# Thirteen units per MLP in place of twelve, with the residual normed and added to in place

## The chip, the core and the metric

The kernel runs on one core of a Trainium2 chip. Its engines are TensorE (PE in the profile, with its weight loads as PEld), VectorE (DVE), ScalarE (ACT), GpSimd (POOL) and SyncE (SP), which issues the loads. The metric is the device time of one execution in microseconds. Each run reports the median of several executions.

## The reference

Sixteen meta tokens and 512 input tokens (528 rows of 1024) go through two layers. Each layer has a mixer and an MLP, and each of these ends in a residual and a LayerNorm:

```python
def sq_relu_mlp(h, w1, w2):
    return jnp.square(jax.nn.relu(h @ w1)) @ w2

    h = layer_norm(DN_ALPHA * h + mix, ln1_w[i], ln1_b[i])
    h = layer_norm(DN_ALPHA * h + sq_relu_mlp(h, mlp_w1[i], mlp_w2[i]), ln2_w[i], ln2_b[i])
```

`w1` is 1024 x 4096 and `w2` 4096 x 1024. The mixer of the first layer is retention and gated DeltaNet heads with one output projection, that of the second is Mamba-2. All is float32. The output drops the meta tokens.

## The kernel before

Activations lie transposed, features on the 128 partitions and tokens along the row. `h` is eight tiles of 528 tokens. In the first layer the tokens are cut in halves of 272 and 256, in the second (the meta tokens are no longer needed) in 256 and 256. Each matrix operand is split in a high part (a rounded copy, by ScalarE, L152) and a low part (the rest, by VectorE, L153), and a product is three matmuls: high by high, high by low, low by high (`mm3`, L172 to L174). In the second layer these run over all 512 tokens at once, and over 256 only where the halves are kept apart (`head` and `tail` of `phase`).

An output projection adds its product to `alpha * h` in a tile of its own (`residual`, L362 to L367). Here `h` is there as a high and a low part, so a first addition is two instructions on VectorE. `norm_after` transposes these sums, norms them by rows, transposes them back, and writes the new `h` as high part (ScalarE, L337), a float32 tile (VectorE, L339) and the low part from both (GpSimd or VectorE, L340).

The MLP's 4096 hidden features are eight groups of four tiles of 128. Per group: `h @ w1`, relu and square (L433 to L442), then the product with the group's rows of `w2`, added to the residual (L362). Groups 2 to 7 do the first product in `Unit`s. A unit takes two tiles of `w1` and both halves of the tokens and both halves of the 1024 inputs, as a product of 2 x 2 blocks, and does it with seven block products in place of eight, at the price of sums and differences of the blocks. One unit is 84 matmuls of half the tokens (L500), against 96. The sums of weight blocks are made in the unit (s1 to s4, L473 to L477), those of `h` once per MLP (`combos`, L385 to L401, split at L152 and L153), in 16 tiles. In the profile's names `m` are tiles of 272 columns (24 buffers), `s` tiles of 528 (40), `w` weight tiles (12), `pmm` and `pmx` PSUM tiles (3 and 5 banks).

The order of the work is that of the program: functions written as generators (`combos`, a unit's preparation, the norm) are advanced a step at each `tick` between products, and a scheduler then sets each engine's queue, in which instructions run in order. Groups 0 and 1 are done tile by tile: four tiles of group 0, then each tile of group 1 followed by two tiles of group 0's second product, whose weights are loaded as they are needed. During these the sums over `h` are made. Then units of two tiles and `Four`s (four tiles of a second product, their weights loaded and split one stage ahead) take turns, and group 7's second product ends the MLP tile by tile, the last three tiles with their halves apart (`tail=3`), so that the first half's norm can start. In the last norm (`finish`) the rows go out to memory.

Of the kernel before, what the change touches and what calls it, by code (L numbers as in the profile page):

```python
# [57 lines left out]
def trunk(ctx: ExitStack, tc: tile.TileContext, a, out):  # L58
# [250 lines left out]
    def norm_after(r, ns, wcol, bcol):  # L309
# [5 lines left out]
        def task(hf):  # L315
# [11 lines left out]
            for m in range(KT):  # L327
# [10 lines left out]
                t = tl("m", n)  # L338
# [33 lines left out]
    def combos(pairs, nh, get):  # L372


        q = slice(0, nh), slice(nh, 2 * nh)

        def part(k, c, lo):
            return pairs[k][lo][:, q[c]].bitcast(F32)

        def diff(out, a, b, engine):  # L380
            engine.tensor_tensor(out, a, b, op=SUB)

        for k in range(4):
            d1, d3, e = tl("m", nh), tl("m", nh), tl("m", nh)
            G.tensor_tensor(d1, part(k, 1, 0), part(k, 0, 0), op=SUB)  # L385
            V.tensor_tensor(e, part(k, 1, 1), part(k, 0, 1), op=SUB)
            V.tensor_tensor(d1, d1, e, op=ADD)
            get(0, k, d1)
            yield
            G.tensor_tensor(d3, part(k + 4, 1, 0), part(k, 1, 0), op=SUB)  # L390
            V.tensor_tensor(e, part(k + 4, 1, 1), part(k, 1, 1), op=SUB)
            V.tensor_tensor(d3, d3, e, op=ADD)
            get(2, k, d3)
            yield
            d2, d4 = tl("m", nh), tl("m", nh)
            G.tensor_tensor(d2, part(k + 4, 1, 0), d1, op=SUB)
            V.tensor_tensor(d2, d2, part(k + 4, 1, 1), op=ADD)
            get(1, k, d2)
            yield
            G.tensor_tensor(d4, part(k + 4, 0, 0), d2, op=SUB)  # L400
            V.tensor_tensor(d4, d4, part(k + 4, 0, 1), op=ADD)  # L401
            get(3, k, d4)
            yield

    def mlp(l, hx, ns, ready, r, evac0, pairs):
# [41 lines left out]

        def second(c, u, m0, m1, tail=0):
            phase([([lambda m=m: wload(second_src(c, m), 512)], m) for m in range(m0, m1)], u,
                  lambda m, hf, o: evac0(m, hf, o, last=c == NG - 1), ns, tail=tail)  # L450
# [110 lines left out]
        u, ev = group()  # L561
        phase([([w1[l, f]], f) for f in range(GF)], hx, ev, ns, head=3, ready=ready)
        spawn(combos(pairs, nh, get))
        stages = []
        un, evn = group()
        groups = [(u, ev), (un, evn)] + [group() for _ in range(2, NG)]
        for c in range(2, NG):
# [947 lines left out]
```

## Time and profile before

| | us |
|---|---|
| median of three runs (1734.0 to 1739.5) | 1738.64 |
| the profiled execution | 1738.46 |
| its span, first to last instruction | 1736.7 |
| TensorE busy | 1674.2 (96%) |
| VectorE busy | 1199.8 (69%) |
| ScalarE busy | 700.9 (40%) |
| GpSimd busy | 351.1 (20%) |
| mean granted clock of TensorE | 0.982 |

The first MLP is from about 535 to 918 us of the span, the second from about 1365 to the end, with the last norm behind it. Busy time on TensorE is pipelined: matmuls overlap, and what counts is how often one starts. "PEclk" is the granted clock as a share of full speed. A wait "X <- Y" is idle time of X before an instruction that Y released. In the tables by stretch each engine has its busy time in us and in brackets the number of instructions that ended or ran in it.

### The profile page before, as it was taken

The numbers are of one execution on the slowest core, as the hardware profiler recorded it, in microseconds if no ns is written. First come the engines' busy times: TensorE is split into PE (matmuls) and PEld (weight loads), VectorE is DVE, ScalarE is ACT, GpSimd is POOL, SyncE is SP. The second block draws the span as 40 slices with busy tenths as digits, with TensorE's granted clock in tenths as the row PEclk, the third lists the DMA queues.
The fourth block names the chain that finished last, engine by engine and source line by source line (L and its number), as shares of the span: only waits on it lengthen the run. The fifth ranks groups of instructions, "written<-read, shape, count | busy, mean of one in ns | idle before, by whom it ended". The sixth has DMA issues, their size and how long they took to land.

```text
span 1736.7 us, 30064 instructions
## 1 busy us (share of the span) xinstructions
PE 1674.2 (96%) x11896; PEld 1542.2 (89%) x11896; DVE 1199.8 (69%) x2383; ACT 700.9 (40%) x1354; POOL 351.1 (20%) x412
## 2 busy tenths in 40 slices
PE   9998999999999899999999998999999998999997
PEld 7897998899999889999998987888778987888886
DVE  5896666766437877767747876767564688777765
ACT  4432235554214344444424643545432434444431
POOL 1211210010003411111102145344410342111112
PEclk9998999999999999999999999999999999999999
DMA  7223212112222232222221443333223123222321
GB/s 243 82 91 86 88 47 84 46 54 84 87 74 68 73 104 98 98 98 98 79 71 62 137 121 92 102 112 98 91 67 110 55 91 110 98 98 98 101 73 69
DMA packets 93002, 158.05 MB, mean 91 GB/s; under 512 B 14077, under 2 KB 47229, under 8 KB 92605
## 3 DMA queue, kind: packets, MB, share of 16 engines
q1 hardware_dynamic: 92716, 155.87, 27.9%
q8 instruction: 93, 1.52, 0.4%
q14 instruction: 49, 0.39, 0.1%
q10 hardware_dynamic: 144, 0.26, 0.0%
HBM read 149.95 MB, written 6.15 MB: 90 GB/s over the span
## 4 chain that ended last, share of the span: by engine, by line
PE 79%; DVE 10%; DMA 4%; POOL 3%; ACT 2%; issue 2%; SPq 0%; POOLq 0%; DVEq 0%; ACTq 0%
PE pmm L172 18%; PE pmm L174 18%; PE pmm L173 18%; PE pmx L500 10%; PE pmm L500 4%; DVE w L153 2%; DVE s L603 2%; DMA row<-rd 1%; DMA w<-in_w 1%; PE pmx L1241 1%; PE pmx L270 1%; DMA du<-row 1%; POOL n L147 1%; PE pmx L1245 1%; ACT w L152 1%
## 5 line engine op out<-in xcount | busy, mean ns | idle before, releaser
L172 PE MATMUL pmm<-hh,w 128*128 128x256 f32 (+5 forms) x1528 | 472.9, 310 | 5.6 <-DVE m L366 2.8
L174 PE MATMUL pmm<-hh,w 128*128 128x256 f32 (+5 forms) x1528 | 459.4, 301 | 2.1 <-DVE w L153 2.1
L173 PE MATMUL pmm<-hl,w 128*128 128x256 f32 (+5 forms) x1528 | 458.4, 300 | 0.7 <-POOL hl L340 0.3
L153 DVE TENSOR_TENSOR w<-w,w 128x1024 fp32r<-128x1024 f32 (+2 forms) x269 | 323.7, 1205 | 142.0 <-PE pmm L173 67.6
L152 ACT CAST w<-w 128x1024 fp32r<-128x1024 f32 (+2 forms) x269 | 263.7, 981 | 373.7 <-PE pmm L174 137.1
L172 PE MATMUL pmm<-s,w 128*128 128x256 f32 (+2 forms) x1180 | 376.8, 319 | 4.3 <-DVE m L366 2.7
L174 PE MATMUL pmm<-s,w 128*128 128x256 f32 (+2 forms) x1180 | 375.5, 318 | 0.2 <-DVE w L153 0.2
L173 PE MATMUL pmm<-s,w 128*128 128x256 f32 (+2 forms) x1180 | 375.5, 318 | 0.0
L172 PEld LDWEIGHTS pmm<-hh,w 128*128 128x128 f32 (+2 forms) x1528 | 289.1, 189 | 20.9 <-issue 4.0
L173 PEld LDWEIGHTS pmm<-hl,w 128*128 128x128 f32 (+2 forms) x1528 | 289.0, 189 | 13.5 <-issue 2.4
L174 PEld LDWEIGHTS pmm<-hh,w 128*128 128x128 f32 (+2 forms) x1528 | 289.0, 189 | 11.4 <-DVE w L153 2.9
L172 PEld LDWEIGHTS pmm<-s,w 128*128 128x128 f32 x1180 | 222.3, 188 | 20.1 <-DVE m L366 3.2
L174 PEld LDWEIGHTS pmm<-s,w 128*128 128x128 f32 x1180 | 222.2, 188 | 15.8 <-DVE w L153 0.6
L173 PEld LDWEIGHTS pmm<-s,w 128*128 128x128 f32 x1180 | 222.2, 188 | 15.2 <-DVE s L1320 0.3
L435 POOL TENSOR_TENSOR m<-m 128x256 f32<-128x256 f32 (+2 forms) x128 | 89.0, 697 | 511.7 <-ACT m L433 499.4
L362 DVE TENSOR_TENSOR m<-m,pmm 128x256 f32<-128x256 f32 (+1 forms) x236 | 93.6, 416 | 71.7 <-PE pmm L174 71.5
L147 POOL TENSOR_TENSOR n<-n,neg 128x1 f32<-128x1 f32 (+2 forms) x58 | 39.8, 690 | 450.4 <-DVE n L146 426.4
L603 DVE SCALAR_TENSOR_TENSOR s<-s,pp,s 128x528 f32<-128x528 f32 x120 | 101.3, 844 | 33.4 <-ACT s L601 31.1
L442 DVE TENSOR_TENSOR s<-m,s 128x256 fp32r<-128x256 f32 (+2 forms) x128 | 69.5, 546 | 51.1 <-POOL m L435 49.9
L500 PE MATMUL pmx<-s,s 128*128 128x264 f32 (+1 forms) x576 | 75.4, 287 | 5.6 <-ACT s L152 5.3
L500 PEld LDWEIGHTS pmx<-s,s 128*128 128x128 f32 x576 | 72.5, 192 | 6.1 <-ACT s L152 5.5
L500 PE MATMUL pmx<-s,w 128*128 128x264 f32 (+1 forms) x576 | 77.6, 284 | 0.0
(312 smaller groups left out, 2368.1 us busy)
## 6 DMA issues: line engine op xcount, KB each, us to landing
w<-in_w SPq DMA_DIRECT2D x88, 512.0 KB, 3.3
w<-in_mw SPq DMA_DIRECT2D x176, 256.0 KB, 3.0
w<-in_mw SPq DMA_DIRECT2D x40, 512.0 KB, 3.2
w<-in_wo SPq DMA_DIRECT2D x29, 512.0 KB, 3.4
row<-rd SPq DMA_DIRECT2D x16, 512.0 KB, 5.7
s<-rd SPq DMA_DIRECT2D x32, 128.0 KB, 5.5
out<-row SPq DMA_DIRECT2D x7, 256.0 KB, 2.0
w<-in_wo SPq DMA_DIRECT2D x6, 256.0 KB, 2.5
```

The source lines that it names most:

```text
L147: G.tensor_tensor(dst, t, neg5[0:part, 0:n], op=POW)
L152: S.copy(dst_hi, src)
L153: V.tensor_tensor(dst_lo, src, dst_hi.bitcast(F32), op=SUB)
L172: T.matmul(o, w[0], x[0], start=first, stop=False)
L173: T.matmul(o, w[0], x[1], start=False, stop=False)
L174: T.matmul(o, w[1], x[0], start=False, stop=last)
L270: T.transpose(pt[m // 4][:bn, (m % 4) * P:(m % 4 + 1) * P], r[m][:, off:off + bn], ident)
L362: V.tensor_tensor(t, t, o, op=ADD)
L435: G.tensor_tensor(q, t, t, op=MUL)
L442: V.tensor_tensor(lo, q, hi.bitcast(F32), op=SUB)
L500: T.matmul(o, w[x][:, c], B[b][k][y], start=first and k == i == 0, stop=last and k == 3 and i == 2, skip_group_check=True)
L603: V.scalar_tensor_tensor(acc, cin[:, k:k + L], w[k], acc, op0=MUL, op1=ADD)
```

## The change

- `norm_after` writes the normed float32 tile over the residual sum that it normed, so that from an output projection to the end of its MLP `h` stays in the same 16 `m` tiles in float32.
- The MLP's residual (`accumulate`) adds to these tiles in place: a first addition is one instruction (`alpha * h + o`), later ones are an addition as before.
- `combos` takes its differences from the float32 tiles, all on VectorE. With halves of 272 and 256 the four token blocks are cut at 264, so a block can lie in two tiles and a difference can be two instructions, one of them 8 columns wide. GpSimd has no part in it.
- In group 1 only tiles 0 and 2 are done directly, one after the other; tiles 1 and 3 are a thirteenth unit. Group 0's second product becomes two `Four`s behind that unit. The later stages follow as before.
- Group 7's second product takes the weights of two `Four`s that are prepared ahead, and keeps the halves of the last four tiles apart (`tail=4`).

```diff
@@ norm_after
-                t = tl("m", n)
+                t = r[hf][m]
                 V.tensor_scalar(t, pf, w, b, op0=MUL, op1=ADD)
@@
+    def accumulate(h):
+        r, seen = [{}, {}], set()
+
+        def evac(m, hf, o, last=True):
+            t = h[hf][m]
+            if (m, hf) in seen:
+                V.tensor_tensor(t, t, o, op=ADD)
+            else:
+                V.scalar_tensor_tensor(t, t, DN_ALPHA, o, op0=MUL, op1=ADD)
+                seen.add((m, hf))
+            if last:
+                r[hf][m] = t
+        return r, evac
+
+    def combos(h, ns, nh, get):
+        def quarter(k, c):
+            a, b = h[0][k], h[1][k]
+            if c == 0:
+                return [(0, nh, a[:, 0:nh])]
+            cut = ns[0] - nh
+            return ([(0, cut, a[:, nh:ns[0]])] if cut else []) + [(cut, nh, b)]
+
+        def diff(out, x, y):
+            if not isinstance(y, list):
+                y = [(0, nh, y)]
+            for o, e, ap in x:
+                for o2, e2, ap2 in y:
+                    lo, hi = max(o, o2), min(e, e2)
+                    if lo < hi:
+                        V.tensor_tensor(out[:, lo:hi], ap[:, lo - o:hi - o], ap2[:, lo - o2:hi - o2], op=SUB)
         for k in range(4):
...
+            q0, q1 = [[quarter(i, c) for c in range(2)] for i in (k, k + 4)]
+            d = [tl("m", nh) for _ in range(4)]
+            diff(d[0], q0[1], q0[0])
+            diff(d[2], q1[1], q0[1])
+            diff(d[1], q1[1], d[0])
+            diff(d[3], q1[0], d[1])
+            for j in range(4):
+                get(j, k, d[j])
+                if j % 2:
+                    yield
@@ mlp
-        for c in range(2, NG):
-            for i in range(2):
-                stages.append(Unit(c, i, lambda f, hf, o, e=groups[c][1]: e(f, hf, o, nh)))
-                stages.append(Four(c - 1, groups[c - 1][0], 4 * i))
-        for f in range(GF):
-            phase([([w1[l, GF + f]], f)], hx, evn, ns)
-            if f == 2:
-                spawn(stages[0].gen)
-            second(0, u, 2 * f, 2 * f + 2)
+        stages = [unit(1, 1), four(0, 0), four(0, 1)]
         for c in range(2, NG):
+            stages += [unit(c, 0), four(c - 1, 0), unit(c, 1), four(c - 1, 1)]
+        last = [four(NG - 1, 0), four(NG - 1, 1)]
...
+        phase([([w1[l, f]], f) for f in range(GF)], hx, groups[0][1], ns, head=3, ready=ready)
+        spawn(combos(h, ns, nh, get))
+        phase([([w1[l, GF]], 0)], hx, groups[1][1], ns)
+        spawn(gens[0])
+        phase([([w1[l, GF + 2]], 2)], hx, groups[1][1], ns)
...
-        second(NG - 1, groups[-1][0], 0, KT, tail=3)
+        blks = last[0].blks + last[1].blks
+        phase([([[blks[m]]], m) for m in range(KT)], groups[-1][0], evac0, ns, tail=4)
@@ both layers
-    h = hn
-    r, ev = residual(h, (0, 0), ns0)
+    h, r0 = hn, r
+    r, ev = accumulate(r0)
```

Behind `combos` the lines of the changed kernel have higher numbers: L442 is L455 there, L473 to L477 are L482 to L486, L500 is L509; the sums' differences are L404, the first residual addition L381.

More of the change, by code (lines that the diff above doesn't have):

```diff
@@ L370, in residual @@
         return r, evac
[L372 to L381, printed above, removed]
-        for k in range(4):
[L384 to L403, printed above, removed]
@@ L409, in mlp @@
+    def mlp(l, hx, h, ns, ready, evac0, pairs):
         w1, w2 = a["mw1"], a["mw2"]
@@ L446, in second_src @@
             return w2[l, c // 2, m][:, c % 2 * 512:c % 2 * 512 + 512]
-        def second(c, u, m0, m1, tail=0):
-            phase([([lambda m=m: wload(second_src(c, m), 512)], m) for m in range(m0, m1)], u,
-                  lambda m, hf, o: evac0(m, hf, o, last=c == NG - 1), ns, tail=tail)
         class Unit:
@@ L559, in run, with unit, four @@
                             adv()
[L561 to L566, printed above, removed]
-        for c in range(2, NG):
-            for i in range(2):
-                stages.append(Unit(c, i, lambda f, hf, o, e=groups[c][1]: e(f, hf, o, nh)))
-                stages.append(Four(c - 1, groups[c - 1][0], 4 * i))
-        for f in range(GF):
-            phase([([w1[l, GF + f]], f)], hx, evn, ns)
-            if f == 2:
-                spawn(stages[0].gen)
-            second(0, u, 2 * f, 2 * f + 2)
+        groups = [group() for _ in range(NG)]
+        def unit(c, i):
+            return Unit(c, i, lambda f, hf, o: groups[c][1](f, hf, o, nh))
+        def four(c, i):
+            return Four(c, groups[c][0], 4 * i)
+        stages = [unit(1, 1), four(0, 0), four(0, 1)]
+        for c in range(2, NG):
+            stages += [unit(c, 0), four(c - 1, 0), unit(c, 1), four(c - 1, 1)]
+        last = [four(NG - 1, 0), four(NG - 1, 1)]
+        gens = [st.gen for st in stages + last]
+        phase([([w1[l, f]], f) for f in range(GF)], hx, groups[0][1], ns, head=3, ready=ready)
[3 more added lines that the diff above has]
+        phase([([w1[l, GF + 2]], 2)], hx, groups[1][1], ns)
         until(lambda: "s4" in stages[0].ops and all(x is not None for y in tt for x in y))
@@ L578, in mlp @@
               [half(k, 1) for k in range(4, 8)], tt[3], tt[0], tt[1], tt[2]]
-        next(stages[1].gen)
+        next(gens[1])
         for i, st in enumerate(stages):
-            nxt = stages[i + 1].gen if i + 1 < len(stages) else iter(())
-            if i + 2 < len(stages):
-                next(stages[i + 2].gen)
+            if i + 2 < len(gens):
+                next(gens[i + 2])
             def adv():
-                next(nxt, None)
+                next(gens[i + 1], None)
                 tick()
             st.run(adv)
-            for _ in nxt:
+            for _ in gens[i + 1]:
                 pass
-        second(NG - 1, groups[-1][0], 0, KT, tail=3)
+        for _ in gens[-1]:
+            pass
+        blks = last[0].blks + last[1].blks
+        phase([([[blks[m]]], m) for m in range(KT)], groups[-1][0], evac0, ns, tail=4)
     def conv_evac(cin, hf, o):
@@ L1365, in trunk @@
     phase([(srcs[m], m) for m in range(3, KT)], yw, ev, ns1, tail=1)
-    h = hn
-    r, ev = residual(h, (0, 0), ns1)
+    h, r0 = hn, r
+    r, ev = accumulate(r0)
     normed = [False, False]
```

5 lines of the change are left out of this document (2 added, 3 removed).

## The prediction

> **What bounds the kernel now.** I read the page first, then busy time by stretch at the head of each MLP, then what TensorE waited for there, then the rows of those stretches in order of time.
>
> ```profile
> PE 1674.2 (96%) x11896; PEld 1542.2 (89%) x11896; DVE 1199.8 (69%) x2383; ACT 700.9 (40%) x1354; POOL 351.1 (20%) x412
> PE 79%; DVE 10%; DMA 4%; POOL 3%; ACT 2%; issue 2%; SPq 0%; POOLq 0%; DVEq 0%; ACTq 0%
> ```
>
> TensorE is the bound nearly everywhere. A change pays by taking matmuls away or by closing the few places where TensorE stands still.
>
> ```profile
> core 0: us, PE busy (x) PEld busy (x) DVE busy (x) ACT busy (x) POOL busy (x), PEclk, DMA share, GB/s
> 640.00:680.00 40.00, 40.00 (x330) 40.00 (x329) 28.77 (x51) 15.05 (x27) 4.46 (x7) 1.00 0.27 93
> 566.87:627.57 60.70, 51.35 (x387) 49.70 (x385) 49.94 (x96) 22.21 (x47) 22.01 (x25) 0.94 0.24 77
> 590.00:600.00 10.00, 8.55 (x68) 8.13 (x67) 10.00 (x23) 3.84 (x9) 4.36 (x6) 1.00 0.01 2
> 614.32:619.21 4.89, 4.89 (x23) 4.89 (x23) 1.62 (x2) 0.00 (x0) 0.00 (x0) 0.51 0.16 54
> 1391.05:1436.06 45.01, 44.81 (x194) 35.97 (x193) 39.90 (x80) 18.92 (x42) 20.51 (x22) 1.00 0.30 100
> ```
>
> The first row is the steady middle of the first MLP: 330 matmuls in 40 us, 0.121 us each, no gap. The second is its head, from the first tile of group 1 to the first of the twelve units: 384 matmuls by the code, which at 0.121 us are 46.5 us, took 60.7. So 14.2 us were lost. Where they were lost VectorE was full (10.00 of 10 us), and then the clock stood at 0.51 for 4.9 us.
>
> ```profile
> PE pmm L172 <- DVE m L366: 5.6, 5, 1.5
> PE pmm L174 <- DVE w L153: 1.9, 1, 1.9
> PE pmm L172 <- ACT m L433: 1.6, 1, 1.6
> PE pmx L330 <- DVE row L322: 0.9, 1, 0.9
> PE pmx L330 <- ACT row L321: 0.7, 1, 0.7
> PE pmx L500 <- ACT s L152: 5.3, 1, 5.3
> PE pmx L270 <- DVE m L362: 1.8, 1, 1.8
> ```
>
> These are TensorE's waits: the first five in 560 to 930 us (first MLP and the norm behind it), the last two from 1350 us on. L366 is the first residual addition of a tile: VectorE is too late to free a PSUM bank. The 5.3 us is the second MLP's first unit, waiting for the last of the h sums. The 1.8 us lies at the very end.
>
> **The change, part by part.** *Matmuls.* A unit does two tiles of w1 in 84 matmuls of half width instead of 96. One more unit per MLP takes 12 away. Rows that give the pitch in the second MLP and mark the stretches:
>
> ```profile
> 566.87 0.29 PE L172 MATMUL pmm<-hh,w 128*128 128x272 f32 x1
> 572.74 0.29 PE L172 MATMUL pmm<-s,w 128*128 128x272 f32 x1
> 614.32 0.43 PE L172 MATMUL pmm<-hh,w 128*128 128x272 f32 x1
> 614.54 0.43 PE L173 MATMUL pmm<-hl,w 128*128 128x272 f32 x1
> 1391.05 0.39 PE L172 MATMUL pmm<-hh,w 128*128 128x512 f32 x1
> 1396.60 0.39 PE L172 MATMUL pmm<-s,w 128*128 128x512 f32 x1
> 1436.06 0.28 PE L500 MATMUL pmm<-hh,w 128*128 128x256 f32 x1
> 1437.36 0.28 PE L500 MATMUL pmm<-hh,w 128*128 128x256 f32 x1
> 1442.93 0.79 PE L500 MATMUL pmx<-s,s 128*128 128x256 f32 x2 [5.30 <-ACT s L152]
> 1444.00 2.50 PE L500 MATMUL pmx<-s,s 128*128 128x256 f32 x10 [0.27 <-DVE s L153]
> 1442.93:1447.15 4.22, 3.95 (x16) 3.65 (x17) 4.22 (x10) 2.79 (x5) 0.00 (x0) 0.50 0.00 0
> ```
>
> A direct tile of the first MLP takes 572.74 - 566.87 = 5.87 us. In the second MLP 24 matmuls of 512 take 5.55 us (0.231 each) and 12 of 256 start 11 pitches in 1.30 us (0.118). At the low clock the pitch is 0.22 in place of 0.12.
>
> The new head of the first MLP has two direct tiles, one unit and all of group 0's second products: 96 + 84 + 192 = 372 matmuls, 45.1 us. In the second it is 48 + 96 = 144 wide ones (33.3 us) and 84 of 256 (9.9 us), 43.2 us.
>
> *VectorE's chain in front of the unit.* Before, the sums over h had the whole head as cover, mixed with 32 residual instructions (L366 and L367) per MLP and 16 subtractions on GpSimd. Now one instruction per tile half does the residual, it stands behind the unit, and the sums are VectorE's alone. But the unit comes after only two direct tiles. Its product s2 needs the second sum of all four k, and the low part of s2. On VectorE, the end of that run in the first MLP (`s_7095` is the last sum it needs, `s_7099` the low part of s2):
>
> ```order
> L153 TENSOR_TENSOR s_7095<-m_7082,s_7095 128x264
> L153 TENSOR_TENSOR w_7164<-w_7120,w_7163 128x1024
> L153 TENSOR_TENSOR s_7099<-w_7009,s_7098 128x512
> L153 TENSOR_TENSOR s_7102<-m_7083,s_7102 128x264
> L153 TENSOR_TENSOR s_7105<-m_7084,s_7105 128x264
> ```
>
> In the kernel before, residual additions and just-in-time weight splits stood between the unit's own preparations at this place:
>
> ```order
> L477 TENSOR_TENSOR s_7387<-w_7360,w_7363 128x512
> L367 SCALAR_TENSOR_TENSOR m_7409<-hl_6432,m_7409 128x272
> L366 SCALAR_TENSOR_TENSOR m_7427<-hh_6431,pmm_7414 128x256
> L153 TENSOR_TENSOR w_7437<-w_7434,w_7436 128x1024
> L367 SCALAR_TENSOR_TENSOR m_7427<-hl_6432,m_7427 128x256
> ```
>
> These rows have moved behind the unit or are gone. On TensorE, the changed kernel does a11, four matmuls of group 0, a12, and then stands at s2 (`pmx_7133`):
>
> ```order
> L509 MATMUL pmm_7132<-hh_6444,w_7078 128x264
> L509 MATMUL pmx_7133<-s_6910,s_7098 128x264 x2
> L174 MATMUL pmm_7269<-s_6559,w_7164 128x272
> L172 MATMUL pmm_7269<-s_6651,w_7163 128x272
> ```
>
> The third matmul of s2 needs `s_7099`. What VectorE's instructions cost (two of POOL beside them):
>
> ```profile
> 546.72 0.14 DVE L146 TENSOR_SCALAR n<-n 128x1 f32<-128x1 f32 x1
> 546.78 0.15 DVE L306 SCALAR_TENSOR_TENSOR n<-n,n 128x1 f32<-128x1 f32 x1
> 571.35 0.98 DVE L442 TENSOR_TENSOR s<-m,s 128x272 fp32r<-128x272 f32 x1 [2.38 <-POOL m L435]
> 575.58 0.98 DVE L392 TENSOR_TENSOR m<-m,m 128x264 f32<-128x264 f32 x1
> 582.39 0.42 DVE L386 TENSOR_TENSOR m<-hl 128x264 f32<-128x264 f32 x1
> 582.73 0.43 DVE L367 SCALAR_TENSOR_TENSOR m<-hl,m 128x272 f32<-128x272 f32 x1
> 603.33 1.21 DVE L153 TENSOR_TENSOR w<-w,w 128x1024 fp32r<-128x1024 f32 x1
> 611.37 0.68 DVE L477 TENSOR_TENSOR s<-w,w 128x512 f32<-128x512 f32 x1
> 1398.96 0.95 DVE L442 TENSOR_TENSOR s<-m,s 128x256 fp32r<-128x256 f32 x1 [0.51 <-POOL m L435]
> 575.34 0.94 POOL L396 TENSOR_TENSOR m<-hh,m 128x264 f32<-128x264 f32 x1
> ```
>
> A half-width instruction starts every 0.35 us (0.42 long), but takes 0.98 beside a GpSimd one. 512 columns cost about 0.6, 1024 about 1.14. For the eight-column slivers, which the trace lacks, the nearest row is the 128x1 with a pitch of 0.06; with a wait for the row before it perhaps 0.16; I take 0.1.
>
> First MLP: group 1's first tile starts at 566.87 and its first low part at 571.35, 4.48 later. The second tile starts at 572.74, so its own is at 577.2 and done at 577.6. Behind it up to `s_7099` stand 22 half-width rows (11 sums, 10 splits, 1 evacuation), 7 slivers, two of 512 and one of 1024: 7.7 + 0.7 + 1.2 + 1.1 = 10.7, so 588.3. TensorE ends the tile at 578.6; a11, a12 and the four matmuls are 3.4 us, some 0.3 goes on a weight cast queued behind an activation: 582.3. Two matmuls of s2 and five others hide 0.85. The wait is 5.2 us. With four GpSimd squarings each stretching a row by 0.55 it is 7.4; I take 6.4. The clock then falls as after 614, 23 matmuls at 0.1 us too much, 2.4. So 45.1 + 0.3 + 6.4 + 2.4 = 54.2 against 60.7: **6.5 us won**.
>
> Second MLP: no slivers. The second low part of the first tile is at 1398.96 to 1399.9, 8.85 after the tile's start; for the next tile that is 1405.45. Then 15 half-width rows, two of 512 and one of 1024, 7.4: 1412.9. TensorE, from 1402.15, has a11, a12, four wide and here twenty more wide matmuls, 8.4 us, and two of s2: 1410.8. The wait is 2.1, with slow rows 3.5; I take 2.75, and half a clock drop, 1.0. Before: 45.0, then 5.57 of waits and over 4 us at a clock of 0.50, some 20 matmuls at 0.1 too much, 2.0: 52.6. After: 43.2 + 3.75 = 46.95. **5.6 us won**.
>
> The Trainium skill ("TensorE: Matmul & The Clock Gate", Part 1) says that the clock halves after an idle window of about 3.4 us, and that the window is free-running. By it alone the second MLP's gap would cost no clock, and the sum would be 1.0 better. The trace is harsher: before the low clock at 614 the longest single wait was 1.9 us, and several of them did it.
>
> *The last group.* Its weights are loaded and split as pairs ahead, and four tiles instead of three do their second halves last. So 12 matmuls of 256 (1.4 us) move behind the first half's norm. At the first MLP's end the waits on L322 and L321 were 0.9 + 0.7; the 1.4 us stand ahead of them now and leave about 0.25: **1.35 won**. At the program's end VectorE gets to the last two additions 1.4 us earlier, with one addition more in front (0.35): **1.1 won**, less 0.05 for the twice 256 columns.
>
> *At nothing:* the norm's writing into the sums' own tiles (their transposes are done); 16 `m` buffers held longer, since the other 8 served the same traffic before, from the residuals' start (if activations had to wait for GpSimd's 0.65 to 0.95, three free PSUM banks cover it); the same bytes of weights in fewer splits.
>
> Sum: 6.5 + 5.6 + 1.35 + 1.05 = 14.5. The profiled execution is 1738.46 (span 1736.7), the median 1738.64. **Forecast 1724 us.**
>
> **The rivals.** (a) *The clock holds* in both heads, and the low clock after the first MLP disappears. Against it are the gap of over 5 us and the low clock from 1442.93 behind one of 5.3. The gain is 2.4 + 1.0 and some 3 more: 1718.
> (b) *The slow form rules*: waits at 7.4 and 3.5, plus 2 us each for ScalarE's casts, which alternate with VectorE's splits, and a full clock drop in both. That takes 1.0 + 0.75 + 4 + 1.0: 1731.
> (c) *The wait only moves*: 6.5 and 5.6 us more of it than I count eat both heads' gain and leave 2.4: 1736, no change. For it speaks that VectorE was the late engine there before, too; against it that it loses 32 rows and GpSimd's company.
> (d) *Slower, by the weights.* On VectorE the unit's first differences of weights now stand in the same queue ahead of the sums, and wait for two loads whose buffers come free only as TensorE finishes the tiles of group 0. In this stretch the weights came none too early:
>
> ```profile
> 558.35 0.62 ACT L152 CAST w<-w 128x512 fp32r<-128x512 f32 x1 [2.03 <-DMA w<-in_mw]
> 569.62 0.62 ACT L152 CAST w<-w 128x512 fp32r<-128x512 f32 x1 [1.72 <-DMA w<-in_mw]
> ```
>
> If the two land 10 us behind the last evacuation of group 0 in both MLPs, every sum moves by that much or a little more: with 24 us in all, 24 - 14.5 makes it 1748. It decides from about 7 us per MLP. Against it: each of these casts had stood idle for 2 us only.
>
> **How the numbers follow.** Forecast 48%, (a) 20%, (b) 20%, (c) 7%, (d) 5%. What a measurement can tell from no change is 0.3%, 5.2 us: below 1733.4 is faster. Forecast and (a) are, and nearly all of (b): 0.87; same 0.08; slower 0.05. The range leaves out half of (a)'s better end, (c) and (d): 1715 to 1733.
>
> **What would show it.** Right: no wait on the residual additions in the heads, one wait of 5 to 7 us at the first unit's s2 in the first MLP and one of 2 to 3.5 in the second, waits at L330 behind the first MLP nearly gone, 12 matmuls fewer per MLP. Wrong: a wait at s2 over 10 us, VectorE idle at the first weight difference, or a new gap in the second products, where the residual additions and the next unit's preparation now meet.

## The result, and the profile after

The changed kernel took 1722.36 us, the median of four runs (1720.05 to 1724.06), against 1736.56 (1734.0 to 1739.5) before: ratio 0.9917, 95% interval 0.9894 to 0.994. A second set of four runs, beside other kernels, gave 1724.21 and 0.9926 (0.9901 to 0.9951). The forecast was 1724, range 1715 to 1733. The profiled execution was the fastest of its four, 1720.05 us with a span of 1718.3, so its 18.4 us against the profile of before are more than the 14.2 between the medians. The profile of the second set is its fastest run too (1719.78, in a set that reaches to 1727.63), so what follows from these two profiles shows the change at its best.

Busy time and the chain by engine, from the page of the changed kernel:

```profile
PE 1663.8 (97%) x11932; PEld 1535.2 (89%) x11932; DVE 1177.9 (69%) x2355; ACT 702.2 (41%) x1346; POOL 325.2 (19%) x380
PE 82%; DVE 7%; DMA 3%; POOL 3%; ACT 2%; issue 2%; SPq 0%; POOLq 0%; DVEq 0%; ACTq 0%
```

VectorE has 28 rows and 21.9 us of work less, GpSimd 32 rows and 25.9 us. VectorE's share of the chain of waits fell from 10 to 7%. TensorE's rows are 36 more: a unit in the second MLP puts 84 matmuls of 256 columns in the place of 48 of 512 (9.9 us in place of 11.1), one in the first 84 in the place of 96, and 12 wide ones of the last group are now 24.

TensorE's waits, first from 535 to 935 us (first MLP and the norm behind it), then from 1350 us on; columns are total, times, longest, in us:

```profile
PE pmx L509 <- ACT s L152: 3.2, 1, 3.2
PE pmx L330 <- ACT row L321: 0.9, 1, 0.9
PE pmx L330 <- DVE n L306: 0.9, 2, 0.5
PE pmm L173 <- POOL hl L340: 0.8, 2, 0.6
PE pmm L174 <- DVE w L153: 0.7, 1, 0.7
...
PE pmx L509 <- DVE s L153: 1.3, 1, 1.3
PE pmx L509 <- ACT s L152: 1.1, 1, 1.1
PE pmm L173 <- POOL hl L340: 1.0, 1, 1.0
PE pmx L270 <- DVE m L379: 0.9, 2, 0.6
```

In the heads no wait stands on the first residual addition any more. A wait at the first unit's s2 (L509) has come, 3.2 us in the first MLP and 2.4 in the second. Two rows are new that the prediction does not have: matmuls of group 0 that wait for a low part of the norm (`hl`, L340) from GpSimd, 0.8 and 1.0 us.

The first MLP's head by stretch: all of it, as in the row of before that starts at 566.87 (its columns are named there), and four microseconds behind the wait:

```profile
565.39:617.91 52.52, 47.88 (x374) 46.95 (x373) 40.03 (x94) 23.15 (x48) 7.53 (x9) 0.97 0.31 101
586.00:590.00 4.00, 3.61 (x19) 3.62 (x20) 4.00 (x8) 2.31 (x6) 0.00 (x0) 0.59 0.35 108
```

The head is 52.5 us long in place of 60.7, VectorE busy for 40 us in place of 50, and the clock falls behind the wait, but only for about 3 us.

The rows of TensorE, ScalarE and VectorE at s2, each in order of time:

```profile
579.29 0.39 PE L172 MATMUL pmm<-s,w 128*128 128x272 f32 x1 [0.53 <-ACT w L152]
580.23 0.39 PE L509 MATMUL pmm<-hh,w 128*128 128x264 f32 x1 [0.19 <-ACT row L513]
585.18 0.51 PE L509 MATMUL pmx<-s,s 128*128 128x264 f32 x2 [3.23 <-ACT s L152]
586.39 0.59 PE L174 MATMUL pmm<-s,w 128*128 128x272 f32 x1 [0.69 <-DVE w L153]
587.69 3.56 PE L509 MATMUL pmx<-s,s 128*128 128x264 f32 x22
...
583.37 0.41 ACT L152 CAST s<-m 128x264 fp32r<-128x264 f32 x1 [1.97 <-DVE m L404]
584.20 0.41 ACT L152 CAST s<-m 128x264 fp32r<-128x264 f32 x1 [0.41 <-DVE m L404]
584.52 0.61 ACT L152 CAST s<-w 128x512 fp32r<-128x512 f32 x1
...
585.12 1.21 DVE L153 TENSOR_TENSOR w<-w,w 128x1024 fp32r<-128x1024 f32 x1
586.26 0.68 DVE L153 TENSOR_TENSOR s<-w,s 128x512 fp32r<-128x512 f32 x1
```

The last row is `s_7099`. It starts at 586.26 and the next row at 586.86, and the prediction's 588.3, moved by the 1.48 us that this head starts earlier, is 586.8. The chain was counted right; what it costs TensorE was not. The prediction has TensorE stop at the third matmul of s2, for `s_7099`. It stopped at the first, for the high part of s2: that cast (584.52) stands in ScalarE's queue behind casts of the sums over `h`, and these waited for VectorE's differences (1.97 and 0.41 us). So VectorE's chain reached TensorE by way of ScalarE's queue, and earlier than by the row that the prediction named. The 0.69 us are a matmul of group 0 that waits for the split at 585.12.

Where the time went, stretch by stretch. "Won" is for equal work: with four last tiles 12 matmuls of 256 columns, 1.4 us, have moved from ahead of each last norm to behind its start, and that is taken into account. "Again" is a second profile of the changed kernel.

| stretch | before, us | after, us (again) | won, us (again) | forecast |
|---|---|---|---|---|
| first MLP, group 0 | 26.92 | 27.67 (27.67) | -0.75 (-0.75) | 0 |
| its head, to the second unit's place | 60.70 | 52.52 (52.78) | 8.2 (7.9) | 6.5 |
| its end, to the next stage's first matmul | 4.56 | 4.95 (4.95) | 1.0 (1.0) | 1.35 |
| next stage, up to its first full-width tile | 9.33 | 6.47 (6.46) | 2.9 (2.9) | 0 |
| second MLP, group 0 | 26.2 | 27.3 (27.3) | -1.05 (-1.05) | 0 |
| its head, to the second products behind the first later unit | 63.52 | 57.54 (56.2) | 6.0 (7.3) | 5.6 |
| end of the program, from the last norm's first sum | 13.67 | 13.98 (13.99) | 1.1 (1.1) | 1.05 |

That is 17.4 us (in the second profile 18.4); the other 1 us lies in stages that the change does not touch. Those vary by more than that: the 14 profiles of this study reach the first MLP after 537.7 to 541.2 us, and need 442.6 to 448.8 us from its end to the second one.

### The profile page after: what moved, and what is told of

Read it like the earlier page. It is cut to its first block, busy times and chain, and to the rows that moved or that the text cites. A ratio compares the mean times of both kernels' runs of the same rounds, so it can differ in the third digit from the quotient of the medians.

```text
span 1718.3 us, 30052 instructions
## 1 busy us (share of the span) xinstructions
PE 1663.8 (97%) x11932; PEld 1535.2 (89%) x11932; DVE 1177.9 (69%) x2355; ACT 702.2 (41%) x1346; POOL 325.2 (19%) x380
## 4 chain that ended last, share of the span: by engine, by line
PE 82%; DVE 7%; DMA 3%; POOL 3%; ACT 2%; issue 2%; SPq 0%; POOLq 0%; DVEq 0%; ACTq 0%
PE pmm L172 19%; PE pmm L174 19%; PE pmm L173 19%; PE pmx L509 11%; PE pmm L509 4%; DVE s L617 2%; DMA row<-rd 1%; DVE w L153 1%; DMA w<-in_w 1%; PE pmx L270 1%; DMA du<-row 1%; POOL hl L340 1%; PE pmx L1259 1%; PE pmx L1255 1%; POOL n L147 1%
## 5 line engine op out<-in xcount | busy, mean ns | idle before, releaser
L172 PE MATMUL pmm<-hh,w 128*128 128x256 f32 (+4 forms) x1480 | 454.6, 308 | 1.6 <-ACT w L152 1.4
L173 PE MATMUL pmm<-hl,w 128*128 128x256 f32 (+3 forms) x1480 | 441.3, 299 | 2.5 <-POOL hl L340 1.9
L174 PE MATMUL pmm<-hh,w 128*128 128x256 f32 (+3 forms) x1480 | 441.7, 299 | 0.5 <-DVE w L153 0.5
L153 DVE TENSOR_TENSOR w<-w,w 128x1024 fp32r<-128x1024 f32 (+2 forms) x253 | 318.4, 1259 | 139.8 <-PE pmm L173 68.9
L172 PEld LDWEIGHTS pmm<-hh,w 128*128 128x128 f32 (+2 forms) x1480 | 278.1, 188 | 15.5 <-issue 4.5
L173 PEld LDWEIGHTS pmm<-hl,w 128*128 128x128 f32 (+1 forms) x1480 | 278.1, 188 | 14.7 <-POOL hl L340 3.2
L174 PEld LDWEIGHTS pmm<-hh,w 128*128 128x128 f32 (+1 forms) x1480 | 277.8, 188 | 8.6 <-DVE w L153 0.9
L448 POOL TENSOR_TENSOR m<-m 128x256 f32<-128x256 f32 (+2 forms) x128 | 90.9, 711 | 545.8 <-ACT m L446 545.5
L147 POOL TENSOR_TENSOR n<-n,neg 128x1 f32<-128x1 f32 (+2 forms) x58 | 39.8, 690 | 442.6 <-DVE n L146 421.7
L455 DVE TENSOR_TENSOR s<-m,s 128x256 fp32r<-128x256 f32 (+2 forms) x128 | 66.5, 522 | 45.7 <-POOL m L448 41.0
L509 PE MATMUL pmx<-s,s 128*128 128x264 f32 (+1 forms) x624 | 81.8, 288 | 5.6 <-ACT s L152 4.3
L509 PEld LDWEIGHTS pmx<-s,s 128*128 128x128 f32 x624 | 78.9, 193 | 6.4 <-ACT s L152 4.9
L509 PE MATMUL pmm<-hh,w 128*128 128x264 f32 (+1 forms) x416 | 83.5, 283 | 0.2 <-ACT row L513 0.2
```

The lines of the kernel that those rows point to most:

```text
L147: G.tensor_tensor(dst, t, neg5[0:part, 0:n], op=POW)
L153: V.tensor_tensor(dst_lo, src, dst_hi.bitcast(F32), op=SUB)
L172: T.matmul(o, w[0], x[0], start=first, stop=False)
L173: T.matmul(o, w[0], x[1], start=False, stop=False)
L174: T.matmul(o, w[1], x[0], start=False, stop=last)
L448: G.tensor_tensor(q, t, t, op=MUL)
```

## Experiments

Each kernel is timed against the kernel before on the same chip (medians of before 1736.6 to 1737.7). The stretches in the table come from the traces: the first MLP from its first matmul to the first row of the norm behind it (L330), the stage between the MLPs, and the second MLP up to TensorE's last matmul; the 10.7 us or so behind that are the same in all. A stretch is from one profile, a median from four runs or more (ten with three last tiles), so the columns need not add up to the difference of the medians.

| kernel | median, us | ratio (95%) | first MLP | between | second MLP |
|---|---|---|---|---|---|
| before | 1736.6 | 1 | 377.7 | 447.2 | 361.2 |
| the change | 1722.4 | 0.9917 (0.9894 to 0.994) | 369.0 | 445.4 | 355.5 |
| the change again | 1724.2 | 0.9926 (0.9901 to 0.9951) | 369.2 | 443.5 | 354.2 |
| in-place sums only | 1728.0 | 0.9935 (0.991 to 0.9959) | 372.2 | 442.7 | 356.3 |
| sums over h only | 1718.5 | 0.9894 (0.9878 to 0.9909) | 366.7 | 447.6 | 352.6 |
| both, old order | 1716.5 | 0.9878 (0.9855 to 0.9901) | 364.8 | 446.0 | 353.6 |
| new order only | 1755.5 | 1.0106 (1.0081 to 1.0132) | 384.3 | 448.5 | 369.6 |
| three last tiles | 1728.0 | 0.9946 (0.9932 to 0.9961) | 371.8 | 448.8 | 356.6 |
| eight rows more | 1727.5 | 0.9943 (0.9923 to 0.9962) | 371.1 | 447.7 | 356.0 |
| s2's sums first | 1724.8 | 0.9926 (0.9906 to 0.9946) | 368.4 | 445.6 | 358.2 |
| four products first | 1716.3 | 0.988 (0.9853 to 0.9907) | 362.9 | 447.0 | 351.4 |
| fresh buffers for the norm | 1721.9 | 0.9907 (0.9887 to 0.9927) | 368.5 | 445.5 | 354.7 |
| four first and fresh | 1712.4 | 0.9862 (0.9843 to 0.9881) | 362.1 | 448.8 | 350.2 |
| twelve units, fresh, four last | 1708.8 | 0.9838 (0.9824 to 0.9853) | 362.7 | 442.7 | 351.8 |

### The change taken apart: rows or order

**Both, old order.** The sums and the residual of the change, in the order of before:

```diff
-        stages = [unit(1, 1), four(0, 0), four(0, 1)]
...
-        phase([([w1[l, GF]], 0)], hx, groups[1][1], ns)
-        spawn(gens[0])
-        phase([([w1[l, GF + 2]], 2)], hx, groups[1][1], ns)
+        for f in range(GF):
+            phase([([w1[l, GF + f]], f)], hx, evn, ns)
+            if f == 2:
+                spawn(stages[0].gen)
+            second(0, u, 2 * f, 2 * f + 2)
...
-        phase([([[blks[m]]], m) for m in range(KT)], groups[-1][0], evac0, ns, tail=4)
+        second(NG - 1, groups[-1][0], 0, KT, tail=3)
```

> The changed kernel's in-place sums and its sums over h from the six residual tiles, but in the order of the kernel before: twelve units per MLP, groups 0 and 1 tile by tile, three last tiles. Theory: the heads were late by VectorE's rows (16 residual rows fewer per MLP at 0.35 us, 8 rows of the sums fewer, no GpSimd row beside them), so most of the two heads' gain of 8.2 and 6.0 us in the traces is kept, less 2 x 1.45 us for the matmuls: about 11 us won, 1725 to 1728. Rival: what pays is the order (the sums and the unit ahead of the residual rows, 12 matmuls fewer per MLP): at most 3 us won, 1733 to 1737.

It took 1716.5 us, faster than either expected time and faster than the whole change. The theory had named the right cause and still taken the order's effect for a gain. The next two kernels show the same from the other side.

**New order only.** The order, 13 units and four last tiles, with the old residual and the old sums over h:

```diff
-        u, ev = group()
...
+        stages = [unit(1, 1), four(0, 0), four(0, 1)]
...
+        spawn(combos(pairs, nh, get))
...
+        phase([([[blks[m]]], m) for m in range(KT)], groups[-1][0], evac0, ns, tail=4)
```

> The reverse: the kernel before with its own residual rows (two per half tile) and its own sums over h (partly on GpSimd), but with 13 units, the new order and four last tiles. Theory (VectorE's rows are the cost): 24 rows of matmuls fewer win 2.9 us, the last group up to 5, but the wait at s2 grows by the sums' 8 more rows (2.8 us) and by GpSimd's company (some 0.5 us on up to 16 rows), 5 us or more per MLP: 1733 to 1740. Rival (the order is what pays): nearly the changed kernel, 1723 to 1727.

It is slower than before, 1755.5 us, and by more than the theory had it. TensorE's waits in the first MLP's head of this kernel:

```profile
PE pmx L500 <- ACT s L152: 7.5, 3, 5.2
PE pmx L500 <- DVE s L153: 3.8, 3, 1.9
```

The unit waits for its sums one product after the other, 11.3 us in six waits, where the changed kernel has one of 3.2 and one of 0.2. So the order of the change can only be borne with the shorter chain on VectorE.

**In-place sums only.** One residual row per half tile in place of two; sums over h and order as before:

```diff
-                t = tl("m", n)
+                t = r[hf][m]
...
-    r, ev = residual(h, (0, 0), ns0)
+    r, ev = accumulate(r0)
```

> The kernel before with the in-place norm and in-place sums alone: one residual row per half tile in place of two; order, sums over h, units and last tiles as before. Theory (VectorE's rows): 16 rows of 0.35 us fewer in each head are worth 4 to 6 us in the first MLP and 1 to 3 in the second, less about 1.8 us of waits on GpSimd's low parts in group 0: 3 to 7 us won, 1730 to 1734. Rival (order): no change, 1735 to 1738.

1728.0 us: the rows count, as the theory has it, and 2 us more came than its range gave.

**Sums over h only.** Residual and order as before; `combos` is that of the change, and the norm keeps its float32 tiles for it:

```diff
-                t = tl("m", n)
+                t = r[hf][m] = tl("m", n)
...
-            G.tensor_tensor(d1, part(k, 1, 0), part(k, 0, 0), op=SUB)
-            V.tensor_tensor(e, part(k, 1, 1), part(k, 0, 1), op=SUB)
-            V.tensor_tensor(d1, d1, e, op=ADD)
...
+            diff(d[0], q0[1], q0[0])
```

> The kernel before (twelve units, old order, three last tiles, two residual rows per half tile) with only the new sums over h: from normed float32 tiles that are kept, all on VectorE, 16 half rows and their eight-column pieces per MLP in place of 24 rows on VectorE and 16 on GpSimd. Theory (a GpSimd row beside VectorE stretches its rows, 0.98 in place of 0.42): 7 to 10 us won over both MLPs, 1727 to 1730, and the stretched rows of 0.8 and more become fewer in the heads. Rival (only the number of rows counts: 8 x 0.35 fewer per MLP less the small pieces): 2 to 4 us, 1733 to 1735. The kept tiles take 16 of the 24 buffers that residual sums and activations use, which can eat part of it.

1718.5 us. This part alone brings about 18 us, twice what the theory gave it. VectorE's groups in the first MLP's head, before and with the new sums only (busy us and mean ns of one, then idle time before):

```profile
L153 DVE TENSOR_TENSOR s<-m,s 128x264 fp32r<-128x264 f32 x16 | 8.1, 512 | 0.5 <-ACT s L152 0.5
L367 DVE SCALAR_TENSOR_TENSOR m<-hl,m 128x272 f32<-128x272 f32 (+1 forms) x15 | 7.5, 499 | 0.1
L442 DVE TENSOR_TENSOR s<-m,s 128x256 fp32r<-128x256 f32 (+1 forms) x9 | 6.6, 729 | 8.6 <-POOL m L435 8.6
```

```profile
L389 DVE TENSOR_TENSOR m<-m,m 128x256 f32<-128x256 f32 (+2 forms) x24 | 6.8, 334 | 0.0
L153 DVE TENSOR_TENSOR s<-m,s 128x264 fp32r<-128x264 f32 x16 | 6.6, 427 | 0.0
L367 DVE SCALAR_TENSOR_TENSOR m<-hl,m 128x272 f32<-128x272 f32 (+1 forms) x15 | 6.3, 429 | 0.2
L440 DVE TENSOR_TENSOR s<-m,s 128x256 fp32r<-128x256 f32 (+1 forms) x9 | 3.9, 430 | 8.9 <-POOL m L433 8.9
```

Rows that this kernel does not touch (`s<-m,s`, `m<-hl,m`) have become shorter: means of 0.50 to 0.73 us fall to 0.43. In this head 14 rows of half width lasted over 0.7 us before, and two more over 0.6; none does now. Those 16 were together 7.7 us longer than rows of 0.43; sixteen subtractions more on VectorE would, at a row every 0.35 us, be an estimated 5.6. So GpSimd's 16 subtractions cost VectorE more than they took off it. This fits the Trainium skill ("SBUF — State Buffer", "SBUF: two separate sides"): a VectorE row with two operands from SBUF and a GpSimd row share a pair of ports as an exclusive lock, and the later one waits for the whole of the other. In the trace of before, the VectorE row of 0.98 us from 571.35 lies over a GpSimd subtraction from 571.28 to 572.04 and ends 0.29 us behind it.

What these heads have in common is seen by stretch: first MLP, fifth direct tile to the first of the twelve later units, for in-place sums only, sums only, and both in the old order (the row of before, 566.87 to 627.57, stands in the prediction):

```profile
568.74:623.14 54.40, 48.92 (x387) 47.35 (x385) 44.81 (x81) 22.05 (x47) 21.18 (x25) 1.00 0.26 85
```

```profile
567.25:617.31 50.06, 47.74 (x386) 47.11 (x385) 39.74 (x100) 21.70 (x47) 8.48 (x9) 1.00 0.29 97
```

```profile
567.82:615.21 47.39, 47.19 (x387) 46.97 (x385) 34.92 (x85) 22.02 (x47) 6.37 (x9) 1.00 0.31 101
```

The third figure of work is VectorE's: 49.9 us before, then 44.8, 39.7 and 34.9. TensorE's 384 matmuls need about 47 us here. As VectorE's work sinks, the head's length sinks from 60.7 to 47.4 us, 0.2 above TensorE's busy time, and the clock stays at 1.00. It is not enough that VectorE's work is less than 47 us: with 44.8 the head is still 54.4. VectorE also stands still, for 8.6 and 8.9 us in the two lists above, in front of rows that wait for GpSimd's squarings. With both parts there is nothing left in the old head for a new order to win but 12 matmuls, 1.45 us. The changed kernel's head, with these 12 matmuls fewer, is 52.5 us.

### What sets the wait in the new head

**Eight rows more.** In front of the sums' low parts VectorE gets eight half-width rows per MLP that change nothing:

```diff
             diff(d[3], q1[0], d[1])
+            for _ in range(2):
+                V.tensor_tensor(d[3], d[3], d[3], op=MAX)
```

> The changed kernel with eight rows more on VectorE per MLP in front of the sums' low parts (each the maximum of a sum with itself, half a tile wide, so nothing else changes). Theory: VectorE's chain in front of s2 sets the wait, so eight rows of 0.35 us move it by 2.8 us in each MLP, from 3.2 + 0.7 to about 6.7 in the first and from 2.3 to about 5.1 in the second, and the low clock behind it grows by up to 1 us each: 1728 to 1730 against 1722.4. Rival: a load or ScalarE's casts set it: 1722 to 1724.

1727.5 us, 3 to 5 us above the two sets of the change, near the theory's lower end; the intervals touch, so the trace has to decide. In the first MLP s2's first matmul starts 22.46 us behind the head's start, in the change 19.79: 2.67 later, against the theory's 2.8. There VectorE's chain does set when s2 can start. The wait itself is 3.69 us, hardly more than before, because TensorE now has 24 matmuls of group 0 ahead of s2 in place of 4; the head is 54.8 us, 2.0 to 2.3 longer. In the second MLP s2's first matmul starts 0.7 us later and its third 0.1 earlier, and the head, measured as in the table above, is 58.2 us, 0.7 to 2.0 longer. There the eight rows do not show in full, and what sets that wait stays open.

**S2's sums first:**

```diff
-            for j in range(4):
+            for j in (1, 0, 2, 3):
                 get(j, k, d[j])
-                if j % 2:
+                if j in (0, 3):
                     yield
```

> The changed kernel with one line of the sums over h in another order: for each k the sum that s2 needs is split first. Theory: the split that s2 needs then stands one row earlier per k, and the scheduler puts four tiles' worth of group 0's matmuls (some 20) ahead of s2 in the first MLP, so the wait of 3.9 and the low clock of 1.2 us there are hidden by 2.4 us and more: 2 to 4 us won, 1718 to 1720. Rival: the wait moves to s3 and s1, whose sums are now later: 1721 to 1724.

1724.8 us, the rival's figure, though the wait did not move to s3 and s1. TensorE has 24 matmuls of group 0 ahead of s2, 4 in the change, as the theory says, and still stands at s2, later:

```profile
581.56 0.40 PE L172 MATMUL pmm<-s,w 128*128 128x272 f32 x1 [1.08 <-ACT w L152]
588.56 0.51 PE L509 MATMUL pmx<-s,s 128*128 128x264 f32 x2 [2.00 <-ACT s L152]
590.05 4.47 PE L509 MATMUL pmx<-s,s 128*128 128x264 f32 x22 [0.98 <-DVE s L153]
```

The head is 52.2 us, where it was 52.5. The waits, 4.1 us, now stand in three places; in the second MLP the two at s2 have grown from 2.3 to 3.5 us, and this MLP is 2.7 to 4.0 us longer. Sorting VectorE's rows differently does not help as long as TensorE has so little to do beside them.

**Four products first.** The first four tiles of group 0's second products go ahead of the unit, with s2's sums first:

```diff
-        stages = [unit(1, 1), four(0, 0), four(0, 1)]
+        stages = [four(0, 0), unit(1, 1), four(0, 1)]
...
-        spawn(gens[0])
+        for g in gens[:2]:
+            next(g)
```

> The changed kernel with the first four second products of group 0 put ahead of the first unit, and the sums that s2 needs split first. Theory: 96 matmuls, 11.6 us, now stand between the last direct tile and the unit, longer than the wait and VectorE's four residual rows in them (8 x 0.35 us): the waits at s2 (3.9 and 2.3) and the low clock (1.2 and 1.3) go: 8 to 9 us won, 1713 to 1715. Rival: the residual rows stand in front of the sums and the wait only moves, as in the old residual's case: 1719 to 1724.

1716.3 us, about 6 to 8 below the change; the expected 8 to 9 came nearly. In the two MLPs alone it is 9 to 10 us; the stage between them was longer in this profile. The first MLP's head of this kernel:

```profile
568.92:615.84 46.92, 46.27 (x375) 45.68 (x374) 39.95 (x91) 23.36 (x49) 7.69 (x9) 1.00 0.28 90
```

VectorE's busy time is the same as in the change, 39.95 us against 40.03. Only TensorE's cover for it has grown, by 96 matmuls: 46.9 us in place of 52.5, no wait at s2, clock 1.00.

### The last group, and the norm's buffers

**Three last tiles:**

```diff
-        phase([([[blks[m]]], m) for m in range(KT)], groups[-1][0], evac0, ns, tail=4)
+        phase([([[blks[m]]], m) for m in range(KT)], groups[-1][0], evac0, ns, tail=3)
```

> The changed kernel with three last tiles doing their second halves last instead of four (its 12 matmuls of 256 columns stand ahead of the norm again). By the prediction's terms it is slower than the changed kernel by 1.35 + 1.05 = 2.4 us, 1725. If the clock that held behind the first MLP held because of these 12 matmuls, the low clock of some 6 us is back there and it is slower by about 5, 1727 to 1728. Rival: the waits only move, no difference, 1722.

1728.0 us, 4 to 6 above the change, and the trace has the reason that the expectation names second. The first 18 us behind the first MLP, from L330's first row: before, the change, this kernel, and the new order alone (which has four last tiles):

```profile
917.63:936.00 18.37, 16.65 (x101) 13.85 (x101) 14.11 (x35) 8.45 (x14) 5.68 (x9) 0.81 0.17 58
```

```profile
906.67:925.00 18.33, 16.61 (x124) 14.26 (x124) 14.56 (x38) 10.57 (x18) 6.25 (x9) 1.00 0.12 41
```

```profile
912.72:931.00 18.28, 16.01 (x96) 12.87 (x96) 13.11 (x34) 8.62 (x15) 6.08 (x9) 0.81 0.09 30
```

```profile
923.62:942.00 18.38, 17.02 (x105) 14.19 (x104) 13.46 (x35) 8.37 (x14) 5.68 (x8) 0.81 0.12 43
```

The clock is 0.81 with three last tiles and 1.00 in the change; at 0.81 between 19 and 28 matmuls and transposes fewer are done in the same time. The last row warns: with the same four last tiles the clock was 0.81 too. Over all profiles the first full-width tile of the next stage began 6.45 to 6.47 us behind that stage's first matmul in seven of the nine with four last tiles, and 7.66 us or later in all five with three and in the other two. The four last tiles make it likely that the clock holds; they do not decide it.

The records of the clock in the traces tell more. In each of the 14 profiles all changes of the clock lie whole multiples of 3.41 us apart, so there is a raster of such steps, and where it lies against the program differs from one execution to the next. With four last tiles the clock held in six profiles in which a step begins 0.0 to 0.7 us behind L330's first row. It fell where one begins 1.9 us (new order only) or 2.3 us (eight rows more) behind it, and held in the ninth, at 2.5. With three it fell at all five places, 0.1 to 2.5 us. At the same place, 0.1 us, it fell with three and held with four, so the 12 matmuls seem to count; whether they are enough goes with the place of the raster. How much work a step must hold is not worked out here.

**Fresh buffers for the norm:**

```diff
-                t = r[hf][m]
+                t = r[hf][m] = tl("m", n)
                 V.tensor_scalar(t, pf, w, b, op0=MUL, op1=ADD)
```

> The changed kernel, but the norm writes each tile into a fresh buffer (which then serves as the sum's tile) instead of the sum's own. GpSimd's order is then again six low parts of the norm and behind them the first squaring; in the changed kernel a squaring of 0.63 us stands ahead of the last two. Theory: that squaring makes the waits on the norm's low parts in group 0 (0.84 and 1.03 us): they go, 1720.5. Rival: 16 buffers held at both ends make activations wait, and the time is the same or 1 to 3 us longer.

GpSimd's rows at the end of the norm ahead of the first MLP, in the change and with fresh buffers (L448 is the squaring of group 0's first tile):

```profile
547.90 3.01 POOL L340 TENSOR_TENSOR hl<-m,hh 128x256 fp32r<-128x256 f32 x4 [2.58 <-DVE m L339]
550.88 0.63 POOL L448 TENSOR_TENSOR m<-m 128x272 f32<-128x272 f32 x1
551.47 1.59 POOL L340 TENSOR_TENSOR hl<-m,hh 128x256 fp32r<-128x256 f32 x2
```

```profile
551.09 4.40 POOL L340 TENSOR_TENSOR hl<-m,hh 128x256 fp32r<-128x256 f32 x6 [2.58 <-DVE m L339]
555.45 2.18 POOL L448 TENSOR_TENSOR m<-m 128x272 f32<-128x272 f32 x3
```

In the change the squaring stands in front of the last two low parts, for which TensorE is waiting. With fresh buffers it stands behind them, as before; group 0 takes 26.92 us again in place of 27.67, and 1.0 us less in the second MLP. In the whole time, 1721.9 against 1722.4 and 1724.2, these 1.75 us cannot be told from no difference. Why a buffer moves the squaring is not shown; it is how the scheduler sets GpSimd's order with the one and the other.

### Faster than both

**Four first and fresh** puts the last two repairs together (the two diffs above):

> The changed kernel with the first four second products ahead of the first unit, s2's sums split first, and the norm writing into fresh buffers. Theory: the two edits add up, 6 us of the first and 1 to 1.8 of the second: 1714 to 1715.5, and no wait on GpSimd's low parts. Rival: the 16 buffers held at both ends now meet the residual rows ahead of the unit and cost the gain again: 1716 to 1719.

1712.4 us: they add up. The 3.9 us below the kernel without fresh buffers are more than the 1.75 expected, but the runs of the two overlap (1711.38 to 1715.11 and 1713.59 to 1719.07).

**Twelve units, fresh, four last.** "Both, old order" with the two small gains:

```diff
-                t = r[hf][m]
+                t = r[hf][m] = tl("m", n)
...
-        second(NG - 1, groups[-1][0], 0, KT, tail=3)
+        second(NG - 1, groups[-1][0], 0, KT, tail=4)
```

> Twelve units and the order of the kernel before, with the in-place sums, the new sums over h, fresh buffers for the norm and four last tiles: only the 13th unit and the new head are taken out. Theory: its heads have no wait (as with three last tiles), so against the head with four second products first it lacks only the 2 x 12 matmuls: 2.9 us more than that one, 1717 to 1718. Rival: the 13th unit's own rows on VectorE (sums of weights, their splits) eat what its matmuls save: the same time, 1714 to 1715.

1708.8 us (1708.24 to 1709.02), the fastest kernel of the study, 0.9838 of before. It is neither the theory's time nor the rival's, and it lies under the kernel above although its matmuls need 2.6 us more (1.45 and 1.2 per unit). The two MLPs themselves are as the theory says: 362.7 + 351.8 us here, 362.1 + 350.2 there, 2.2 us longer. The other way round it is in the stage between them, whose work is the same in both; here, then with four products first:

```profile
901.90:1344.63 442.73, 426.84 (x2816) 369.82 (x2816) 297.03 (x508) 203.33 (x346) 143.32 (x123) 0.99 0.34 100
```

```profile
900.98:1349.76 448.78, 430.01 (x2817) 373.71 (x2816) 296.38 (x506) 201.52 (x344) 144.40 (x123) 0.98 0.32 96
```

6.05 us lie there, in TensorE's busy time (3.2, at a clock of 0.99 against 0.98) and in its idle time (2.9). The larger part can be the clock's: in this stage it stands at half for three steps of 3.41 us here and for six there, and three steps at half cost up to 5.1 us. Over the 14 profiles the six with three or four such steps took 442.6 to 445.6 us in this stage, the eight with five to seven 446.0 to 448.8. No experiment shows why the one kernel has three and the other six. It may be that the end of the MLP sets how that stage begins, or chance; that the four runs of this kernel lie at 1708.24 to 1709.02, and those of the other at 1711.38 to 1715.11, speaks against chance alone. So the 13th unit, which wins about 2 us inside the MLPs, has not been shown to pay in the whole time, even in a head where nothing waits at the unit.

## Why the prediction was right, and where not

**The time and the sum.** 14.5 us were forecast, 14.2 and 12.8 measured between medians. Of its four terms the two heads were a little low (6.5 and 5.6, in the traces 8.2 and 6.0, again 7.9 and 7.3), the ends not far off (1.35 and 1.05 against 1.0 and 1.1). Two things were not in the sum and partly cancel: +2.9 us for the clock behind the first MLP, -1.8 for GpSimd's order. That is luck, and so in part is the first of them. The stretches won add up to 17.4 and 18.4 us, more than the medians' 14.2 and 12.8, because both profiles of the change are the fastest of their sets.

**The head of the first MLP.** The chain up to `s_7099` was right to 0.1 us once its start is set right. That TensorE would stop at the third matmul of s2 was wrong (it stopped at the first, behind ScalarE's queue), and two surcharges were too high. The wait was put at 5.2 us without slow rows and 6.4 was taken; the rows show 3.23 + 0.69 at s2 and 0.53 + 0.19 ahead of it. No half-width row of this head was long, none of 61; of the "four GpSimd squarings each stretching a row by 0.55" one did stretch a row, an eight-column one, from 0.16 to 0.60 us. The low clock was put at 2.4 us. The 27 matmuls from 586.39 to 591.08 took 4.7 us, where at 0.121 they take 3.3: it cost 1.4.

**The head of the second MLP.** Of 2.75 us of wait 2.34 came. Half a clock drop, 1.0 us, was taken. The row of s2 behind the second wait, in the first profile of the change and in the second:

```profile
1402.02 4.23 PE L509 MATMUL pmx<-s,s 128*128 128x256 f32 x22 [1.28 <-DVE s L153]
```

```profile
1403.09 2.88 PE L509 MATMUL pmx<-s,s 128*128 128x256 f32 x22 [1.29 <-DVE s L153]
```

The two steps of the clock's raster in which these waits lie, again in the same order (TensorE's busy time is the first figure behind the length, the clock the third number from the end; in the second profile, where the clock did not change here, the steps' place follows from its changes elsewhere):

```profile
1398.24:1401.65 3.41, 1.44 (x7) 0.71 (x5) 3.41 (x8) 2.80 (x7) 0.00 (x0) 1.00 0.53 156
1401.65:1405.06 3.41, 3.04 (x14) 3.04 (x15) 2.42 (x7) 2.17 (x3) 0.00 (x0) 0.50 0.00 0
```

```profile
1398.37:1401.78 3.41, 2.35 (x11) 1.47 (x9) 3.41 (x10) 1.86 (x6) 0.00 (x0) 1.00 0.40 121
1401.78:1405.19 3.41, 2.12 (x18) 2.10 (x18) 3.41 (x8) 2.92 (x5) 0.00 (x0) 1.00 0.09 35
```

It is the same program with the same two waits (1.06 + 1.28 and 1.06 + 1.29), and the clock is 0.50 for a step in one execution and 1.00 throughout in the other: 22 matmuls take 4.23 us and 2.88. In the first execution most of both waits falls into one step, in which TensorE is busy for 1.44 us of 3.41; the next step runs at half clock. In the second each step has one wait, TensorE is busy for 2.35 and 2.12 us, and the clock holds. So the forecast's half drop was right as a mean of the two, and the length of a gap alone does not decide. This fits the Trainium skill ("TensorE: Matmul & The Clock Gate", Part 1), by which the window that judges TensorE idle runs freely and is about 3.4 us long, as the raster's step is here. Where the Trainium skill puts the half clock behind a whole idle window, the measurement is the harsher one, as the prediction took it: TensorE was busy for 1.44 us in the step before this fall, and for 0.51 us in the step before that of the first MLP (582.46 to 585.87).

**"At nothing: the norm's writing in place."** This step failed. Its direct cost is nothing, but with the change of buffers squarings stand ahead of the norm's last low parts on GpSimd (one ahead of two in the first MLP, two ahead of one in the second), 0.75 and 1.05 us. The order of GpSimd's rows shows it; the prediction argued from TensorE's and VectorE's alone.

**The end of the first MLP.** Its waits did not go as said. Of 0.92 + 0.69 us at L330 one wait of 0.95 us is left, on ScalarE's row (L321), where 0.25 was forecast, and 1.0 us was won in place of 1.35. That the low clock behind it would stay was the assumption of the forecast; it went in both profiles, as rival (a) had it, and by the raster that is in part chance.

**The rivals.** (a) had one of its three pieces in both profiles, the clock behind the first MLP, and the second head's in one of the two; in the first head the clock fell. (b) fell: no slow rows. (c) was nearest to the truth of the order, though it priced it wrongly: the new order does put back a wait, and it costs more than the 13th unit's matmuls save. (d) fell: at the first unit's weight differences VectorE did not wait for loads at all, at the second's for 1.2 us, not 10.

**What the prediction did not ask.** It read the old head rightly as VectorE's, and then priced the whole new head at once: 14.2 us lost there, so much lost here, the difference won. It never asked how the old head would stand with the new rows. That needs only its own rows: VectorE's 49.9 us in that head, less 15 rows of 0.43 (L367), less 8 of the 24 rows of the sums, is 40, without GpSimd's stretching 32 to 35, and TensorE needs 47. With that the old head has no wait, and its 47.4 us are the bar for a new one. The measured split is: rows 12.9 and 7.6 us won in the two MLPs; the order lost 5.6 to 5.8 us in the first and 1.7 to 3.0 in the second (the change's two profiles against "both, old order", for equal work, the four last tiles' 1.1 us at the end left out), with the matmuls that the units save already in it. The net was right because both halves were in the one number.

## What to carry to other kernels

When a change brings lighter work and a new order together, price the old order with the lighter work first: the lighter work may already have taken all that the order was to win, and a new order that shortens the cover over the remaining chain then only costs. Operations moved to a second engine are not gained when they slow the first one's rows: compare the mean of rows that nobody touched. A step on the bound engine is worth covering before it is worth reordering: ahead of the unit 96 matmuls closed a wait that sorting its sums did not. And where a clock is judged on a raster that the program does not choose, one profile of each kernel does not show what an edit does to the clock: two profiles of one program are the least.

## What the runs showed of the hardware

VectorE's half-width rows last 0.42 us alone and up to 0.99 beside GpSimd's two-operand rows; taking 16 GpSimd rows and 8 of VectorE's out of each MLP brought the stretched rows in the first head from 14 to none and was worth 18 us, where 16 residual rows of VectorE's per MLP were worth 9 by the medians and 11 by the ratio (ratios 0.9894 and 0.9935).

Pieces of eight columns are nearly free on VectorE. In the changed kernel's first head:

```profile
567.54 0.16 DVE L404 TENSOR_TENSOR m<-m 128x8 f32<-128x8 f32 x1
567.62 0.50 DVE L404 TENSOR_TENSOR m<-m,m 128x256 f32<-128x256 f32 x2
```

One lasts 0.16 us, and the next row starts 0.08 us behind its start; the estimate was 0.1. One of the twelve, at 578.52, lasted 0.60 us, beside a GpSimd squaring from 578.38 to 579.09.

A stage that no kernel touched was the least steady part: the work between the MLPs took 442.6 to 448.8 us in 14 profiles, and in two profiles of one program 445.4 and 443.5. Its length goes with the number of 3.41 us steps at half clock, three to seven. A difference of a few us in one pair of profiles is therefore not yet a difference of kernels.
